# Tables of 65, 88 and 106 rows padded to 128 in DRAM, and the transforms moved one projection back, in a hybrid Hyena and RG-LRU block

## The chip, the cores and the metric

One core of one Trainium2 chip. The metric is the device time of one execution in microseconds (us), as the median of several runs. The core has a matrix engine (TensorE, PE), VectorE (DVE), ScalarE (ACT), GpSimd (POOL), and SyncE (SP), from whose queue nearly all transfers are issued; sixteen DMA engines move the data.

## What is computed

One layer on 528 positions (16 meta tokens and 512 tokens) of width 1024. Cut to what matters:

```
n    = rmsnorm(h)                                  # 528 x 1024
proj = n @ w_in                                    # hyena v, x1, x0 | rglru x | rglru gate | branch gates
A    = fft_long_conv(v * x1, filter) * x0          # two-sided, length 528, 512 channels
B    = (rglru(x, forward) + rglru(x, backward)) * gelu(gate)
h    = h + (sigmoid(gA) * (A @ hy_out) + sigmoid(gB) * (B @ rg_out)) @ w_out
h    = h + peer(rmsnorm(h))                        # product-key retrieval of experts
out  = rmsnorm(h)[16:]
```

The filter of the convolution comes from a small network (two sine layers of 64 on 528 positions, then 64 to 1024, times an exponential decay). The kernel does the Fourier transforms as matrix products with tables of cosines and sines.

## The kernel before, in words

**Precision and weights.** Every product is done with operands split into a high and a low f16 half: three matmuls for one (`mm3`, lines 84 to 88; lines 86, 87 and 88 are the three). A weight block of 128x1024 f32 (512 KB, `wf`) is loaded from SP's queue, split by ScalarE (line 81, the high half) and VectorE (line 82, the low half), and used by TensorE. `w_load`, `w_prep` and `w_get` (lines 94 to 122) keep this going: three `wf` buffers, so that a load waits until VectorE has split the block three before it, and splits that run two blocks ahead of the projection that asks. A projection's `w_get` puts these splits into ScalarE's and VectorE's queues; each engine works in the order in which its instructions were put there.

**Order of the front.** `front` (from line 284) writes the order out by hand. SP's queue begins with `hs` (the filter network's input and first weights, 65 rows), four parts of `xt` (the activations), the vectors, three `wf`, the identity, `w3` (65 rows) and `dec` (the decay, 106 rows). Then come the norm, and the projections in sequence, each followed by steps of background generators (`proj`, lines 256 to 282, whose last lines step the generators it was given):

- four pairs of projections for v and x1 (line 271, 48 matmuls of 264 columns each). The first pair is done together in both PSUM buffers of its kind, then the next weights are split, and only then are the two evacuated (`pad`, line 406). In the background: the filter network's second layer and `filter_taps` (lines 184 to 222), which multiplies by `dec` and leaves the split taps `pq` (j from 0 to 4, s for the sum and the difference of both directions).
- `filter_dft` (lines 224 to 248): five groups of 30 matmuls, each with its own table `kc` (106 rows), three buffers. The first two tables are asked for after the second pair, the other three when the groups begin. ScalarE evacuates a group (`kri`, line 246).
- four projections for x0, then eight for the gelu gates (24 matmuls of 512 columns each). Each takes one step of `hyena_conv` (lines 591 to 690) and one of `small_params`. The steps of `hyena_conv` are: load `ud` (88 rows) and `iv` (106 rows) and fold the input; three steps of transposes and their splits `eo` (line 612, by way of lines 81 and 82); five steps with a forward transform each (`fwd`, 18 matmuls, `ps_u`), the first of which also holds the last `eo` split, and each later one the product of the transform before (lines 628 to 633, then the split `ri`); the last product; four steps with an inverse transform each (`inv`, 30 matmuls of 264 columns, `ps_y`) and the post-processing of the one before; the last post-processing. The twelve projections take twelve of the fifteen steps; the rest is drained after the last one (lines 460 to 462).
- the RG-LRU projections and scans, the output projections, and then the expert stage (`peer`), which reads 128 expert blocks from two tables and gathers rows, to the end.

PSUM has two buffers for projections and two for everything else in the front (`pg`). The tables `kdft`, `udft`, `idft` and `dec` are made on the host in `constants` (line 1355), `hy_small` (for `hs` and `w3`) in `layout` (line 1397).

Of the kernel before, what the change touches and what calls it, by code (L numbers as in the profile page):

```python
# [8 lines left out]
F32 = mybir.dt.float32  # L9
F16 = mybir.dt.float16  # L10
# [10 lines left out]
L = SEQ + META  # L21
HL = L // 2
EPS = 1e-6
D_HY = 512
FFN = 64
# [3 lines left out]
FN = 5  # L29
FC = 106  # L30
NF = FN * FC
EC = 88
# [34 lines left out]
class Kernel:  # L67
# [156 lines left out]
    def filter_dft(self, p, psum, hy, pq, kri):  # L224
        nc, a = self.nc, self.a
        kcs = []

        def load(f):
            if f < FN:
                kc = p.tile([FC, 2, 2, FN, FC], F16, name="kc", bufs=3)  # L230
                nc.sync.dma_start(kc, a["kdft"][f])
                kcs.append(kc)
        for f in range(2):
            load(f)
        yield
        for f in range(FN):
            load(f + 2)
            kc = kcs[f]
            ps = psum.tile([128, 2, 512], F32, name="ps_kf", tag="pg")
            for s in range(2):  # L240
                for j in range(FN):
                    n = min(FC, L - j * FC)
                    self.mm3(ps[:FC, s, :], kc[:n, s, 0, j, :], kc[:n, s, 1, j, :],
                             pq[:n, s, 0, j, :], pq[:n, s, 1, j, :], j == 0, j == FN - 1)
            kr = hy.tile([FC, 2, D_HY], F32, name="kri", tag="kr", bufs=FN + 1)
            nc.scalar.activation(kr, ps[:FC], AF.Copy, scale=1.0 / (S_K * S_C))
            kri.append(kr)
            yield
# [35 lines left out]
    def front(self, xt, acc):  # L284
        nc, tc, a, keep = self.nc, self.tc, self.a, self.keep
        ctx = ExitStack()
        psum = ctx.enter_context(tc.tile_pool(name="psf", bufs=2, space=PSUM))
# [63 lines left out]
        kri = []  # L351
        pf = ctx.enter_context(ExitStack())
        fp = pf.enter_context(tc.tile_pool(name="filt", bufs=1, side="right"))
        hs = fp.tile([FFN + 1, L + 2 * FFN + 4], F32, name="hs")
        nc.sync.dma_start(hs, a["hy_small"][:, :L + 2 * FFN + 4])
        for c in range(0, 8, 2):
            nc.sync.dma_start(xt[:, c:c + 2, :], a["ht"][:, c:c + 2, :])
# [8 lines left out]
        h1 = fp.tile([FFN, L], F32, name="h1")  # L366
        h2 = fp.tile([FFN + 1, L], F32, name="h2")
        pq = fp.tile([FC, 2, 2, FN, D_HY], F16, name="pq")
        dec = fp.tile([FC, FN, D_HY], F32, name="dec")
        w3 = fp.tile([FFN + 1, 2 * D_HY], F32, name="w3")  # L370
        nc.sync.dma_start(w3, a["hy_small"][:, L + 2 * FFN + 4:])
        nc.sync.dma_start(dec, a["dec"])
        nc.gpsimd.memset(h2[FFN:FFN + 1, :], 1.0)
        mlp = [self.filter_mlp(fp, psum, i, hs, h1, h2) for i in range(2)]
# [40 lines left out]
        bg = self.filter_taps(fp, psum, w3, h2, pq, dec)  # L415
# [32 lines left out]
        sp = self.small_params()  # L448
        bg = self.hyena_conv(psum, hy, u, x0, kri, y_hy)
# [6 lines left out]
            nc.scalar.activation(t, ps[:, 0, :], AF.Gelu_apprx_tanh, scale=1.0 / (S_N * S_W))  # L456
            gelus.append(t)
        for i in range(8):
            self.proj(psum, False, ev_gelu, (bg, sp))
        self.flush_evac()  # L460
        for _ in bg:
            pass
# [8 lines left out]
        with tc.tile_pool(name="ru", bufs=1, side="right") as ru:  # L471
# [17 lines left out]
            bg = self.rglru(ru, psum, rgx, gelus, rgw, y_rg)  # L489
# [36 lines left out]
        for i in range(8):  # L526
            w = self.w_get(self.wi)
# [63 lines left out]
    def hyena_conv(self, psum, hy, u, x0, kri, y_hy):  # L591
        nc, tc, a = self.nc, self.tc, self.a
        with tc.tile_pool(name="hc", bufs=1, side="right") as p:
            ud = p.tile([EC, 2, 2, 3, NF], F16, name="ud")
            nc.sync.dma_start(ud, a["udft"])
            iv = p.tile([FC, 2, 2, FN, HL], F16, name="iv")
            nc.sync.dma_start(iv, a["idft"])
            eo = p.tile([EC, 2, 2, 3, D_HY], F16, name="eo")
            fold = []
            for i in range(4):  # L600
# [64 lines left out]
            for k in range(6):  # L665
# [4 lines left out]
                if k % 2 == 1:  # L670
                    yield
            post()
            post = None
            for f in range(FN):
                nxt = fwd(f)
# [673 lines left out]
def _hl(m, s):  # L1349
    m = np.asarray(m, np.float64) * s  # L1350
    hi = m.astype(np.float16)
    return hi, (m - hi.astype(np.float64)).astype(np.float16)


def constants():
    c = {}
    f = np.arange(NF)
    w = np.pi * f / L
    n = np.arange(NF)
    ok = (f[None, :] <= L)  # L1360
    kd = np.zeros((FC, 2, 2, FN, NF), np.float16)
    for s, fn in enumerate((np.cos, np.sin)):
        m = fn(n[:, None] * w[None, :]) * ok
        for r, v in enumerate(_hl(m, S_C)):
            kd[:, s, r] = v.reshape(FN, FC, NF).transpose(1, 0, 2)
    c["kdft"] = np.ascontiguousarray(kd.reshape(FC, 2, 2, FN, FN, FC).transpose(4, 0, 1, 2, 3, 5))
    m = np.arange(HL) + 0.5
    ud = np.zeros((EC, 2, 2, 3, NF), np.float16)
    iv = np.zeros((FC, 2, 2, FN, HL), np.float16)
    wt = np.where((f == 0) | (f == L), 1.0, 2.0) * (f <= L)  # L1370
    for s, fn in enumerate((np.cos, np.sin)):
        x = fn(m[:, None] * w[None, :]) * ok
        for r, v in enumerate(_hl(x, S_C)):
            ud[:, s, r] = v.reshape(3, EC, NF).transpose(1, 0, 2)
        y = (x * wt[None, :]).T
        for r, v in enumerate(_hl(y, S_C)):
            iv[:, s, r] = v.reshape(FN, FC, HL).transpose(1, 0, 2)
    c["udft"], c["idft"] = ud, iv
    t32 = np.linspace(0.0, 1.0, L, dtype=np.float32)[:, None]
    wz = np.float32(2.0 * math.pi / L) * np.arange(L, dtype=np.float32)[:, None]  # L1380
    bands = np.linspace(1e-4, 15, 16, dtype=np.float32)[None, :]
    ph = (bands * wz).astype(np.float64)
    z = np.concatenate([t32, np.cos(ph), -np.sin(ph)], axis=-1).astype(np.float32)
    zt = np.zeros((FFN + 1, L), np.float32)
    zt[:33] = z.T
    c["zt"] = zt
    deltas = np.abs(np.linspace(math.log(1e-2) / 0.3, math.log(1e-2) / 1.5, D_HY, dtype=np.float32))
    dec = np.zeros((NF, D_HY), np.float32)
    dec[:L] = np.exp((-t32 * deltas).astype(np.float64))
    c["dec"] = np.ascontiguousarray(dec.reshape(FN, FC, D_HY).transpose(1, 0, 2))  # L1390
    c["ident"] = np.eye(128, dtype=np.float32)
    c["iota"] = np.broadcast_to(np.arange(128, dtype=np.float16), (128, 128)).copy()
    c["iof"] = np.broadcast_to(np.repeat(np.arange(TOPK, dtype=np.float16), TOPK), (128, 256)).copy()
    return c


def layout(i):
    i = {k: np.asarray(v) for k, v in i.items()}
    a = {}
    h = np.concatenate([i["meta"], i["x"][0]], axis=0)  # L1400

    def cols(v):
        return np.ascontiguousarray(v.reshape(-1, 128).T)

    a["ht"] = np.ascontiguousarray(h.T.reshape(8, 128, L).transpose(1, 0, 2))
    a["vecs"] = np.concatenate([cols(i[k]) for k in VEC], axis=1)

    def lhs(w):
        k, m = w.shape
        return np.ascontiguousarray(  # L1410
            w.reshape(k // 128, 128, m // 128, 128).transpose(2, 1, 0, 3).reshape(m // 128, 128, k))

    a["gfb"] = np.broadcast_to(i["g_final"], (128, D)).copy()
    a["w_in"] = lhs(i["w_in"][0])
    a["hy_out"] = lhs(i["hy_out"][0])
    a["rg_out"] = lhs(i["rg_out"][0])
    a["w_out"] = lhs(i["w_out"][0])
    a["wq"] = lhs(i["peer_wq"][0])
    a["rg_gate_w"] = np.ascontiguousarray(
        i["rg_gate_w"][0].reshape(32, 128, 128).transpose(1, 0, 2).reshape(128, 32 * 128))  # L1420
    a["keys"] = np.ascontiguousarray(i["peer_keys"][0].reshape(16, 128, 128).transpose(2, 0, 1).reshape(128, 2048))
    a["peer_u"] = np.ascontiguousarray(
        i["peer_u"][0].reshape(128, 128, 8, 128).transpose(0, 3, 2, 1).reshape(128, 128, D))
    a["peer_v"] = np.ascontiguousarray(i["peer_v"][0].reshape(128, 128, D))
    a["peer_un"] = np.ascontiguousarray(i["peer_u"][0])

    def rows(v):
        return np.concatenate([v, np.zeros((FFN + 1 - v.shape[0], v.shape[1]), v.dtype)], axis=0)

    hb = np.stack([i["hy_b1"][0], i["hy_b2"][0], i["hy_freq"][0, 0], i["hy_freq"][0, 1]], axis=1)  # L1430
    c = constants()
    a["hy_small"] = np.concatenate(
        [c.pop("zt"), rows(i["hy_w1"][0]), rows(i["hy_w2"][0]), rows(hb),
         np.concatenate([i["hy_w3"][0], i["hy_b3"][0][None]], axis=0)], axis=1)
    a.update(c)
    return a

# [15 lines left out]
```

## Time and profile before

| | |
|---|---|
| median of 3 runs | 1748.39 us (1746.59 to 1750.73) |
| the profiled execution, its own time | 1748.05 us |
| its span, first to last instruction | 1746.3 us |
| mean granted TensorE clock | 0.975 of full speed |
| PE / DVE / ACT / POOL busy | 93% / 80% / 44% / 21% of the span |
| moved by DMA | 414.33 MB, 237 GB/s over the span |

The profile is of one execution. Busy shares are over the whole span; the stages differ. A row of a timeline gives the start, the duration, the engine, the line of the kernel, the operation, output<-input, shapes, the count and, in brackets, how long the engine was idle before it and what ended that wait. Matmuls overlap one another, so that the distance of two starts tells their pace, and not the duration of one. PEclk is the granted clock of TensorE as a share of 2.4 GHz, and the DMA share is the mean busy share of the sixteen DMA engines.

### The profile page before, as it was taken

To read this page: it belongs to the slowest core of one execution; us is meant where nothing else is said; L and a number is where in the kernel's file an instruction comes from. 1 tells how busy PE (TensorE), PEld (TensorE's weight loads), DVE (VectorE), ACT (ScalarE), POOL (GpSimd) and SP (SyncE) were. 2 spreads that over 40 slices of the span, in tenths; PEclk is the share of its full clock that TensorE was granted. 3 is DMA by queue.
4 is the path that set the end of the run, shared out by engine and by line. 5 is a ranking of instruction groups with operands and counts; after the bars stand their busy time and mean duration, and the time that the engine had idled before them with its cause. 6 is when DMAs were issued, how large, how long until landed. Compare 5 with 4: busy or idle time off the path is not lost. (4 is left out here: it accounts for less than half of the span.)

```text
span 1746.3 us, 25010 instructions
## 1 busy us (share of the span) xinstructions
PE 1630.6 (93%) x9451; PEld 910.5 (52%) x9451; DVE 1403.7 (80%) x2422; ACT 767.6 (44%) x1055; POOL 359.8 (21%) x321
## 2 busy tenths in 40 slices
PE   6987999899989988898999998899999999999898
PEld 4755576544434544565665665455554444444343
DVE  5825768997567899899899797688889999989884
ACT  4323349893243432443654675333333333333342
POOL 0000000000000000222222123344444444444410
PEclk8998999999999999999999999899999999999999
DMA  4214132123323345778787799999999999999981
GB/s 164 93 48 120 63 106 75 61 85 92 114 82 99 97 124 193 244 241 288 272 311 278 282 341 349 340 388 323 344 370 359 402 396 404 399 395 406 395 299 49
DMA packets 134541, 414.33 MB, mean 237 GB/s; under 512 B 11955, under 2 KB 39859, under 8 KB 131047
## 3 DMA queue, kind: packets, MB, share of 16 engines
q1 hardware_dynamic: 97347, 277.87, 45.3%
q0 software_dynamic: 37072, 134.86, 20.6%
q8 instruction: 74, 1.21, 0.3%
q14 instruction: 48, 0.39, 0.1%
HBM read 366.54 MB, written 46.14 MB: 236 GB/s over the span
## 5 line engine op out<-in xcount | busy, mean ns | idle before, releaser
L978 PE MATMUL ob<-wh,pt 128*128 128x512 f16 x2304 | 512.1, 380 | 20.8 <-DVE wh L82 12.0
L82 DVE SCALAR_TENSOR_TENSOR wh<-wf,wh 128x1024 f16<-128x1024 f32 (+1 forms) x340 | 409.3, 1207 | 135.8 <-ACT wh L81 133.3
L81 ACT ACTIVATE wh<-wf 128x1024 f16<-128x1024 f32 (+1 forms) x340 | 352.6, 1041 | 176.6 <-DMA wf<-in_peer_v 58.4
L978 PEld LDWEIGHTS <-pt 128*128 128x128 f16 x2304 | 225.9, 98 | 290.1 <-issue 24.2
L88 PE MATMUL ps_e<-x,wh 128*128 128x384 f16 x1024 | 337.7, 330 | 16.2 <-DVE wh L82 16.2
L86 PE MATMUL ps_e<-x,wh 128*128 128x384 f16 x1024 | 338.2, 330 | 2.3 <-ACT gs L952 2.3
L87 PE MATMUL ps_e<-x,wh 128*128 128x384 f16 x1024 | 337.9, 330 | 0.0
L1092 POOL DMA_INDIRECT rows<-in_peer_un,gidx x128 | 181.4, 1417 | 447.7 <-DVE junk L1125 396.0
L88 PEld LDWEIGHTS <-wh 128*128 128x128 f16 x1504 | 148.6, 99 | 150.1 <-DVE wh L82 23.6
L87 PEld LDWEIGHTS <-wh 128*128 128x128 f16 x1504 | 148.7, 99 | 130.7 <-issue 13.8
L1092 POOL DMA_INDIRECT rows<-in_peer_v,gidx x128 | 171.8, 1342 | 196.5 <-DVE acc L1146 157.4
L86 PEld LDWEIGHTS <-wh 128*128 128x128 f16 x1504 | 148.8, 99 | 121.6 <-issue 6.0
L1146 DVE SCALAR_TENSOR_TENSOR acc<-rows,dots,acc 128x1024 f32<-128x1024 f32 x127 | 162.7, 1281 | 19.2 <-DMA rows<-in_peer_v,gidx 18.3
L940 ACT ACTIVATE pt<-pf 128x384 f16<-128x384 f32 x128 | 66.5, 520 | 218.4 <-DVE pf L933 162.3
L1125 DVE SCALAR_TENSOR_TENSOR junk<-rows,xn 128x1024 f32<-128x1024 f32 x128 | 156.1, 1219 | 4.8 <-DMA rows<-in_peer_un,gidx 4.1
L271 PE MATMUL ps_p<-n,wh 128*128 128x264 f16 x960 | 115.3, 282 | 8.2 <-ACT pad L406 6.8
L271 PEld LDWEIGHTS <-wh 128*128 128x128 f16 x960 | 95.7, 100 | 28.5 <-issue 10.3
L952 ACT ACTIVATE gs<-ps_e 128x384 f32<-128x384 f32 x96 | 47.0, 489 | 133.7 <-PE ps_e L88 124.8
L1287 ACT ACTIVATE stg<-ps_gt 128x512 f32<-128x512 f32 x96 | 93.1, 1082 | 14.1 <-PE ps_gt L1280 10.5
L944 DVE TENSOR_TENSOR pt<-pf,pt 128x384 f16<-128x384 f32 x128 | 70.8, 553 | 12.4 <-ACT pt L940 12.4
L86 PE MATMUL ps_p<-n,wh 128*128 128x512 f16 x192 | 74.0, 386 | 0.0
L87 PE MATMUL ps_p<-n,wh 128*128 128x512 f16 x192 | 73.8, 384 | 0.0
(276 smaller groups left out, 1840.1 us busy)
## 6 DMA issues: line engine op xcount, KB each, us to landing
wf<-in_peer_u SPq DMA_DIRECT2D x128, 512.0 KB
wf<-in_peer_v SPq DMA_DIRECT2D x128, 512.0 KB
gd<-stg SPq DMA_DIRECT2D x24, 1024.0 KB
wf<-in_w_in SPq DMA_DIRECT2D x44, 512.0 KB
gin<-gd SPq DMA_DIRECT2D x7, 3072.0 KB
sd<-gs SPq DMA_DIRECT2D x48, 384.0 KB
sin<-sd SPq DMA_DIRECT2D x48, 384.0 KB
wf<-in_wq SPq DMA_DIRECT2D x16, 512.0 KB
```

Of the source, the lines that this page charges most:

```text
L81: self.nc.scalar.activation(hi, src, AF.Copy, scale=s)
L82: self.nc.vector.scalar_tensor_tensor(lo, src, s, hi, op0=OP.mult, op1=OP.subtract)
L86: mm(ps, lh, rh, start=first, stop=False)
L87: mm(ps, lh, rl, start=False, stop=False)
L88: mm(ps, ll, rh, start=False, stop=last)
L271: nc.tensor.matmul(ps[:, h, :HL], x, n[:, y, c, h * HL:(h + 1) * HL], start=(c == 0 and x is lh and y == 0), stop=(c == 7 and x is ll))
L944: nc.vector.tensor_tensor(pt[i][:, 1, :], pf.pop(i), pt[i][:, 0, :], OP.subtract)
L978: mm(ob[tt][:, h, :], pp[:, x, sl], w[:, y, h * 512:(h + 1) * 512], start=first and k == 0, stop=last and k == 2)
L1092: self.nc.gpsimd.indirect_dma_start(out=r, out_offset=None, in_=table, in_offset=bass.IndirectOffsetOnAxis(ap=self.gidx[:, j:j + 1], axis=0))
L1125: nc.vector.scalar_tensor_tensor(junk, rows.pop(0), 1.0, self.xn, op0=OP.mult, op1=OP.mult, accum_out=self.dots[:, j:j + 1])
L1146: nc.vector.scalar_tensor_tensor(acc2, r, d, acc2, op0=OP.mult, op1=OP.add)
L1287: nc.scalar.activation(st[c][:, :, o:o + 4].rearrange("p e t -> p t e"), ps, AF.Copy, scale=S_P / S_G)
```

## The change

The four tables are padded with zero rows to 128 in DRAM, and so is `hy_small`; the tiles that they are loaded into have 128 rows, and each load takes the whole table. The computation reads the same rows as before (`w3`, `ud` and `iv` are cut to their rows after the load; the others are addressed by rows already).

`hyena_conv` gets one more step: the last `eo` split is a step of its own, so that the first forward transform comes one projection later. The gelu projections from the fifth on take two steps each, so that all sixteen steps are done when the last projection is. Counted from the last x0 projection, the order on TensorE before was: gelu 0, transform 0, gelu 1, transform 1, gelu 2, transform 2, gelu 3, transform 3, gelu 4, transform 4, gelu 5, gelu 6, inverse 0, gelu 7, inverses 1, 2, 3. After: gelu 0, gelu 1, transform 0, gelu 2, transform 1, gelu 3, transform 2, gelu 4, transforms 3 and 4, gelu 5, inverse 0, gelu 6, inverses 1 and 2, gelu 7, inverse 3.

```diff
--- before.py
+++ after.py
@@ -227,7 +227,7 @@
 
         def load(f):
             if f < FN:
-                kc = p.tile([FC, 2, 2, FN, FC], F16, name="kc", bufs=3)
+                kc = p.tile([128, 2, 2, FN, FC], F16, name="kc", bufs=3)
                 nc.sync.dma_start(kc, a["kdft"][f])
                 kcs.append(kc)
         for f in range(2):
@@ -351,7 +351,7 @@
         kri = []
         pf = ctx.enter_context(ExitStack())
         fp = pf.enter_context(tc.tile_pool(name="filt", bufs=1, side="right"))
-        hs = fp.tile([FFN + 1, L + 2 * FFN + 4], F32, name="hs")
+        hs = fp.tile([128, L + 2 * FFN + 4], F32, name="hs")
         nc.sync.dma_start(hs, a["hy_small"][:, :L + 2 * FFN + 4])
         for c in range(0, 8, 2):
             nc.sync.dma_start(xt[:, c:c + 2, :], a["ht"][:, c:c + 2, :])
@@ -366,9 +366,10 @@
         h1 = fp.tile([FFN, L], F32, name="h1")
         h2 = fp.tile([FFN + 1, L], F32, name="h2")
         pq = fp.tile([FC, 2, 2, FN, D_HY], F16, name="pq")
-        dec = fp.tile([FC, FN, D_HY], F32, name="dec")
-        w3 = fp.tile([FFN + 1, 2 * D_HY], F32, name="w3")
+        dec = fp.tile([128, FN, D_HY], F32, name="dec")
+        w3 = fp.tile([128, 2 * D_HY], F32, name="w3")
         nc.sync.dma_start(w3, a["hy_small"][:, L + 2 * FFN + 4:])
+        w3 = w3[:FFN + 1]
         nc.sync.dma_start(dec, a["dec"])
         nc.gpsimd.memset(h2[FFN:FFN + 1, :], 1.0)
         mlp = [self.filter_mlp(fp, psum, i, hs, h1, h2) for i in range(2)]
@@ -456,7 +457,7 @@
             nc.scalar.activation(t, ps[:, 0, :], AF.Gelu_apprx_tanh, scale=1.0 / (S_N * S_W))
             gelus.append(t)
         for i in range(8):
-            self.proj(psum, False, ev_gelu, (bg, sp))
+            self.proj(psum, False, ev_gelu, (bg, sp) + (bg,) * (i >= 4))
         self.flush_evac()
         for _ in bg:
             pass
@@ -591,10 +592,11 @@
     def hyena_conv(self, psum, hy, u, x0, kri, y_hy):
         nc, tc, a = self.nc, self.tc, self.a
         with tc.tile_pool(name="hc", bufs=1, side="right") as p:
-            ud = p.tile([EC, 2, 2, 3, NF], F16, name="ud")
+            ud = p.tile([128, 2, 2, 3, NF], F16, name="ud")
             nc.sync.dma_start(ud, a["udft"])
-            iv = p.tile([FC, 2, 2, FN, HL], F16, name="iv")
+            iv = p.tile([128, 2, 2, FN, HL], F16, name="iv")
             nc.sync.dma_start(iv, a["idft"])
+            ud, iv = ud[:EC], iv[:FC]
             eo = p.tile([EC, 2, 2, 3, D_HY], F16, name="eo")
             fold = []
             for i in range(4):
@@ -670,6 +672,7 @@
                 if k % 2 == 1:
                     yield
             post()
+            yield
             post = None
             for f in range(FN):
                 nxt = fwd(f)
@@ -1388,6 +1391,11 @@
     dec = np.zeros((NF, D_HY), np.float32)
     dec[:L] = np.exp((-t32 * deltas).astype(np.float64))
     c["dec"] = np.ascontiguousarray(dec.reshape(FN, FC, D_HY).transpose(1, 0, 2))
+
+    for k, ax in (("kdft", 1), ("udft", 0), ("idft", 0), ("dec", 0)):
+        w = [(0, 0)] * c[k].ndim
+        w[ax] = (0, 128 - c[k].shape[ax])
+        c[k] = np.pad(c[k], w)
     c["ident"] = np.eye(128, dtype=np.float32)
     c["iota"] = np.broadcast_to(np.arange(128, dtype=np.float16), (128, 128)).copy()
     c["iof"] = np.broadcast_to(np.repeat(np.arange(TOPK, dtype=np.float16), TOPK), (128, 256)).copy()
@@ -1432,6 +1440,7 @@
     a["hy_small"] = np.concatenate(
         [c.pop("zt"), rows(i["hy_w1"][0]), rows(i["hy_w2"][0]), rows(hb),
          np.concatenate([i["hy_w3"][0], i["hy_b3"][0][None]], axis=0)], axis=1)
+    a["hy_small"] = np.pad(a["hy_small"], ((0, 128 - FFN - 1), (0, 0)))
     a.update(c)
     return a
```

## Rows read from the trace of the kernel before

**Rows 1.** The page, the span in 40 equal slices: busy share of the DMA engines, in tenths.

```profile
DMA  4214132123323345778787799999999999999981
```

**Rows 2.** Waits of TensorE, 0 to 260 us: in total, times, longest.

```profile
PE ps_u L86 <- ACT eo L81: 8.8, 1, 8.8
...
PE ps_kf L86 <- DMA kc<-in_kdft: 5.0, 2, 4.1
```

**Rows 3.** Timeline of ScalarE: start, duration, work, idle before and what ended it.

```profile
39.92 1.06 ACT L81 ACTIVATE wh<-wf 128x1024 f16<-128x1024 f32 x1 [8.26 <-DMA wf<-in_w_in]
40.88 0.59 ACT L406 ACTIVATE pad<-ps_p 128x528 f32<-128x528 f32 x1
...
164.93 1.06 ACT L81 ACTIVATE wh<-wf 128x1024 f16<-128x1024 f32 x1 [14.82 <-DMA wf<-in_w_in]
```

**Rows 4.** DMA issues: what, queue, count, size of each.

```profile
kc<-in_kdft SPq DMA_DIRECT2D x5, 438.9 KB
...
iv<-in_idft SPq DMA_DIRECT2D x1, 1093.1 KB
dec<-in_dec SPq DMA_DIRECT2D x1, 1060.0 KB
...
hs<-in_hy_small SPq DMA_DIRECT2D x1, 167.6 KB
```

**Rows 5.** Stretches: us, engines' busy time, then granted clock, DMA share, GB/s.

```profile
10.00:12.00 2.00, 2.00 (x6) 1.50 (x5) 0.71 (x1) 0.94 (x3) 0.00 (x0) 1.00 1.01 414
...
108.00:112.00 4.00, 4.00 (x20) 2.40 (x19) 0.00 (x0) 0.34 (x1) 0.00 (x0) 1.00 0.13 53
156.00:160.00 4.00, 3.02 (x14) 1.65 (x13) 0.00 (x0) 0.00 (x0) 0.00 (x0) 1.00 0.12 53
...
102.20:107.20 5.00, 5.00 (x12) 2.56 (x13) 0.00 (x0) 0.00 (x0) 0.00 (x0) 0.50 0.13 53
```

**Rows 6.** Timeline of SP's queue: when tables are issued.

```profile
89.80 8.48 SPq L231 DMA_DIRECT2D kc<-in_kdft  x3
...
129.86 0.25 SPq L597 DMA_DIRECT2D iv<-in_idft  x1
```

**Rows 7.** Timeline of TensorE: 96 projection matmuls, at three places.

```profile
21.64 13.09 PE L271 MATMUL ps_p<-n,wh 128*128 128x264 f16 x96
...
41.53 13.32 PE L271 MATMUL ps_p<-n,wh 128*128 128x264 f16 x96 [6.81 <-ACT pad L406]
...
236.87 10.97 PE L271 MATMUL ps_p<-n,wh 128*128 128x264 f16 x96
```

**Rows 8.** Timeline: the filter transform's first matmul, and a split that it needs.

```profile
84.88 0.38 PE L86 MATMUL ps_kf<-pq,kc 106*106 106x512 f16 x1
...
85.23 0.69 DVE L82 SCALAR_TENSOR_TENSOR pq<-kp,pq 104x512 f16<-104x512 f32 x1 [0.70 <-ACT pq L81]
```

**Rows 9.** Timeline of ScalarE: evacuations after the third and fifth filter groups.

```profile
111.66 1.02 ACT L246 ACTIVATE kri<-ps_kf 106x1024 f32<-106x1024 f32 x1 [12.59 <-PE ps_kf L88]
...
125.73 1.02 ACT L246 ACTIVATE kri<-ps_kf 106x1024 f32<-106x1024 f32 x1 [6.56 <-PE ps_kf L88]
```

**Rows 10.** Timeline of TensorE: first matmuls of forward transforms 0, 1 and 2.

```profile
155.61 0.38 PE L86 MATMUL ps_u<-eo,ud 88*106 88x512 f16 x1
...
176.73 0.38 PE L86 MATMUL ps_u<-eo,ud 88*106 88x512 f16 x1
...
185.80 0.38 PE L86 MATMUL ps_u<-eo,ud 88*106 88x512 f16 x1
```

**Rows 11.** Timeline of VectorE: a product's start, its split, and a weight split.

```profile
208.03 0.69 DVE L628 TENSOR_TENSOR yt<-ps_u,kri 106x512 f32<-106x512 f32 x1 [2.00 <-PE ps_u L88]
...
211.81 1.29 DVE L82 SCALAR_TENSOR_TENSOR ri<-yt,ri 106x512 f16<-106x512 f32 x2
213.35 1.23 DVE L82 SCALAR_TENSOR_TENSOR wh<-wf,wh 128x1024 f16<-128x1024 f32 x1 [0.25 <-ACT wh L81]
```

## The prediction

> **What bounds the kernel now.** TensorE is busy most of the span, and the page's forty slices show the DMA engines near their limit only in the last half [rows 1]. The changed tables are used in the front, the first 250 us, where those engines mostly idle: a wait for a table there can't come from a full memory system. Second I read the list of waits on TensorE up to 260 us: `ps_u` behind ScalarE's `eo` (8.8 us) and `ps_kf` behind the load of `kc` (5.0 us) [rows 2]; a third, 6.81 us, stands before the matmuls at 41.53 [rows 7]. Third, ScalarE's timeline says why two of them exist though they name no DMA: a weight split waited 8.26 us and another 14.82 us for `wf`, and what TensorE needed (`pad`, `eo`) was queued behind it [rows 3].
>
> Why should a `wf` be late when its load is small? Fourth, the stretches. At 108 to 112 and at 156 to 160 us one table alone is moving (`kc`, then `iv`), and the sixteen DMA engines are busy 0.13 and 0.12 of the time at 53 GB/s; at 10 to 12 us, with loads of 128 rows under way, they are all busy (1.01) at 414 GB/s [rows 5]. 0.125 is two engines of sixteen. So I read: a load of 106 rows runs on two engines, and each later load, which has a share on those two, waits behind it. The sizes fit: `kc` is 438.9 KB, 449 thousand bytes, 8.5 us at 53 GB/s; `iv` 21 us, `dec` 20.5 us [rows 4].
>
> **The padding, stall by stall.**
>
> *`dec`, start of the projections.* TensorE ends the first 96 matmuls at 21.64+13.09 = 34.73 and starts again at 41.53 [rows 7], because the `pad` evacuation at 40.88 stands behind the late split [rows 3]. With `dec` on sixteen engines that `wf` is there when ScalarE asks at 39.92-8.26 = 31.7; `pad` then starts at the end of the matmuls, and TensorE 0.65 us later as now, at 35.4: 6.15 us. The next 96 matmuls took 13.32 us, against 10.97 for 96 of the same kind with no pause ahead of them [rows 7]: 2.35 us more for TensorE if the pause goes. But VectorE and ScalarE, whose chain from here to the filter transform has few pauses, gain only the 6.15. What is late next is `pq`: its low half, 85.23+0.69 now, comes at 79.8, while TensorE, 8.5 us earlier than now, wants it 13 matmuls of 0.216 us (rate below) after 84.88-8.5, at 79.2 [rows 8]. With the hand-over that costs 0.7 us: 7.8 us.
>
> *`kc`.* Three of the five tables are issued from 89.80 on [rows 6], in order. A group of 30 matmuls at 0.216 us takes 6.48 us, so ScalarE, after an evacuation of 1.02 us, should wait 5.46 for the next; before the third and the fifth it waits 12.59 and 6.56 [rows 9]: 7.13+1.10 = 8.2 us, idle and slow matmuls together. After: `wf` and `kc`, 1 MB, take 2.5 us at 414 GB/s, 5 at half that; the third group wants it at 111.66-12.59-1.02 = 98.05 in today's times, 8 us after the issue, and both ends move together. Covered; 8.2 us gained.
>
> *`ud`, `iv`.* From the first matmul of transform 0 to that of transform 1 are 21.12 us; from 1 to 2, the same 42 matmuls, 9.07, that is 0.216 each [rows 10]. So 12.05 us go. Padding and reordering serve the same stall: the split that holds up `eo` waited 14.82 us and TensorE only 8.8 [rows 2, 3], so without the late `wf` `eo` is there 6 us before it is wanted, and the added projection (24 x 0.216 = 5.2 us) makes that 11. Counted once.
>
> *Added bytes.* `hs` grows from 65 to 128 rows, 167.6 KB to 330 [rows 4], ahead of `xt` in the queue, and the norm waits for `xt`: 162 KB at 414 GB/s are 0.4 us. Bounds: 0 (it also spreads wider) and 0.8 (half the rate). I take 0.4, by the nearest row. `w3` and `dec` stand behind `xt` and before a `wf` wanted only at 31.7: nothing; without that cover 0.47 MB more, 1.1 us. `ud` and `iv`, issued up to 129.86 [rows 6], are 3 MB when padded, 7 us, before a `wf` wanted at 164.93-14.82 = 150.1 [rows 3]: nothing. Slicing the tiles by rows costs no instruction.
>
> **The reordering.** The new yield moves each transform one projection back, and from the fifth gelu projection on two steps follow each. These steps issue no DMA and nothing on POOL, so SP's order stays; on ScalarE and VectorE they pass weight splits and gelu evacuations. (a) Transforms 3 and 4 run back to back, and the product of 4 has one projection left before the first inverse. A product takes VectorE from 208.03 to 211.81+1.29 = 213.1, its first low half ready after 4.45; a weight split adds 1.23 and its wait 0.25 [rows 11]. Counted from the end of transform 3, that half is ready at 5.3+1.5+4.45 = 11.3; TensorE wants it after 3.9 (transform 4), 5.2 and 13 matmuls of 264 columns at 10.97/96 = 0.114, at 10.6. Cost 0.7 us; bounds 0 and 2.2 (a second split in between). (b) The last gelu evacuation now stands behind the last inverse's post-processing and frees a buffer for the second RG-LRU projection, 5.5 us after: nothing, at most 1. (c) That projection's weight split passes behind two post-processings and still has a gelu projection and an inverse to spare: nothing.
>
> **Sum.** 7.8 + 8.2 + 12.05 - 0.4 - 0.7 = 26.95 us. The profiled execution took 1748.05 (span 1746.3): 1721.1; it stood 0.34 under the median of the runs: 1721.4. Behind the front all work waits for the front's result, and weights come through three buffers, so nothing is fetched sooner that could collide, and the shift passes through whole.
>
> **Rivals.**
>
> *Slower: the rate belongs to these tables, not to their row count.* If such a load gets 53 GB/s at any count, padding stretches it by 128/106. `dec` lands 4.3 us later, three `kc` in a row 5.3, `iv` 4.4, which the added projection hides: 9.6 us slower, 1758. It decides if the padded loads still show a share of 0.13. Against: 128-row loads in the same queue [rows 5]. Chance 0.05. The Trainium skill, "DMA: Bandwidth & Descriptors", section on why a DMA increments its semaphore by 16, gives a DMA the largest number of engines up to 16 that divides its rows: 2 for 106, 11 for 88, 13 for 65, 16 for 128. The trace agrees with the 2.
>
> *No table was late: bytes alone set a load's time, and the waits have another cause.* Then nothing comes back, and `hs` and the reordering cost 0.4+0.7: 1749.5. Against: `kc` was issued from 89.80 and its user was held about 12 us [rows 6, 9], while 414 GB/s would bring it in one. Chance 0.02. The Trainium skill, "DMA: Bandwidth & Descriptors", section on the anatomy of one DMA, has such a rule: about 2.0 us and bytes over 436 GB/s, by which an estimate for `kc` is 3.0 us, and 3.2 padded. The trace disagrees by a factor of four.
>
> *The clock stays down.* After the `kc` pause the granted clock was 0.50 from 102.2 to 107.2 [rows 5], 1.2 GHz. If it falls in these places without the pauses, only idle time comes back; the gain loses 1.65 + (8.2-5.0) + (12.05-8.8) = 8.1 us: 1729.5. Against: matmuls with no pause ahead ran at 0.216 us throughout [rows 10]. Chance 0.1.
>
> *The gain becomes slack.* The last half is near the DMA's limit [rows 1]; if something there kept its own time, the result would be 1748. Against: its loads start only when the front's buffers come free. Chance 0.02.
>
> **Numbers.** Forecast 0.81: 1721.4, and by the bounds above, with a pause more or less that brings the clock down elsewhere (2.35 us, [rows 7]), 1715 to 1728. To hold 8 in 10 the range reaches into the clock's case: 1715 to 1731. 0.2%, about what a measurement of this kernel can tell, is 3.5 us: faster 0.91, same 0.04, slower 0.05.
>
> **What would show it.** Right: no wait for `kc`; no wait of ScalarE over 3 us for `wf` before 200 us; a DMA share near 1 for a few us at each table instead of 0.13 for 8 to 30; the RG-LRU projections from about 210 us instead of 236.87 [rows 7]. Wrong: a share of 0.13 beside padded tables; a new wait of TensorE over 2 us for `pq` or before the first inverse; RG-LRU 27 us earlier, but the end not.

## The result, and the profile after

| | before | after |
|---|---|---|
| median | 1747.49 us (4 runs) | 1717.99 us (4 runs, 1715.17 to 1720.26) |
| the profiled execution, its own time | 1748.05 us | 1716.81 us |
| its span | 1746.3 us | 1715.0 us |
| mean granted clock | 0.975 | 0.982 |

The ratio is 0.9834, 95% interval 0.9817 to 0.9851: 29.5 us faster. The forecast was 1721.4 in a range of 1715 to 1731.

The list of waits on TensorE in the changed kernel, 0 to 245 us (total, times, longest):

```profile
PE ps_f L178 <- ACT h L182: 4.7, 1, 4.7
PE ps_f L178 <- DMA hs<-in_hy_small: 4.1, 1, 4.1
PE ps_p L271 <- DVE wh L82: 2.0, 1, 2.0
PE ps_t L612 <- DVE eo L82: 0.5, 1, 0.5
PE ps_kf L87 <- DVE pq L82: 0.3, 1, 0.3
PE ps_y L88 <- DVE ri L82: 0.3, 1, 0.3
...
```

The waits of 8.8 and 5.0 us [rows 2] and the one of 6.81 [rows 7] are gone. The first four lines stood in the list before too (4.7, 3.4, 1.4 and 0.5 us). In place of the stalls stand the two small ones that the forecast had expected, for `pq` and before an inverse transform, at 0.3 us each.

The timeline of TensorE after, at the places of [rows 7, 8, 10] (start, duration, work):

```profile
20.43 23.05 PE L271 MATMUL ps_p<-n,wh 128*128 128x264 f16 x192
...
73.57 0.38 PE L86 MATMUL ps_kf<-pq,kc 106*106 106x512 f16 x1
...
106.54 10.63 PE L271 MATMUL ps_p<-n,wh 128*128 128x264 f16 x93
...
141.81 0.38 PE L86 MATMUL ps_u<-eo,ud 88*106 88x512 f16 x1
...
150.87 0.38 PE L86 MATMUL ps_u<-eo,ud 88*106 88x512 f16 x1
...
206.40 10.96 PE L271 MATMUL ps_p<-n,wh 128*128 128x264 f16 x96
```

The first two groups of 96 matmuls are now one row of 192, without a pause that the list of waits shows. From transform 0 to transform 1 there are 9.06 us instead of 21.12. The RG-LRU projections begin at 206.40 instead of 236.87, 30.5 us earlier, and the span is 31.3 shorter: what the front gained has arrived at the end.

ScalarE's timeline after, at the places of [rows 3, 9]:

```profile
29.41 1.99 ACT L81 ACTIVATE wh<-wf 128x1024 f16<-128x1024 f32 x2
31.85 0.61 ACT L407 ACTIVATE pad<-ps_p 128x528 f32<-128x528 f32 x1 [0.45 <-PE ps_p L271]
...
93.78 1.02 ACT L246 ACTIVATE kri<-ps_kf 106x1024 f32<-106x1024 f32 x1 [5.46 <-PE ps_kf L88]
...
106.74 1.02 ACT L246 ACTIVATE kri<-ps_kf 106x1024 f32<-106x1024 f32 x1 [5.46 <-PE ps_kf L88]
```

Two weight splits run back to back where 8.26 us lay between them, `pad` waits only for its own matmuls, and the third and fifth evacuations wait the 5.46 us of an undisturbed group.

The stretches of the changed kernel where `dec` moves (14 to 16 us) and where `ud` and then `iv` move (113 to 117, 117 to 119); the last three columns are the granted clock, the DMA share and GB/s:

```profile
14.00:16.00 2.00, 0.00 (x0) 0.00 (x0) 1.79 (x3) 1.39 (x2) 0.00 (x0) 0.94 1.08 455
...
113.00:117.00 4.00, 4.00 (x38) 3.48 (x36) 2.43 (x3) 0.60 (x1) 0.13 (x2) 1.00 1.00 426
...
117.00:119.00 2.00, 2.00 (x20) 1.85 (x18) 0.39 (x1) 1.02 (x2) 0.00 (x0) 1.00 1.00 428
```

The share of 0.13 at 53 GB/s [rows 5] has become 1.0 or a little over at 426 to 455.

To place the gain, I cut the span at five points of TensorE's timeline: the first projection, the first filter tap (`ps_k`, 54.69 before and 43.31 after), the first filter transform, the first x0 projection (125.53 before), the first RG-LRU projection. The same table serves for the experiments. Every number is the length of a stretch in us, from that run's profile. Below, "the `kc` stretch" is the column of the filter transforms, and "the transforms' stretch" the one with x0, gelu and hyena.

| run | start | pairs (`dec`) | taps | filter transforms (`kc`) | x0, gelu, hyena (`ud`, `iv`) | rest | span |
|---|---|---|---|---|---|---|---|
| before | 21.64 | 33.05 | 30.19 | 40.65 | 111.34 | 1509.4 | 1746.3 |
| after | 20.43 | 22.88 | 30.26 | 32.97 | 99.86 | 1508.6 | 1715.0 |
| padding alone | 21.45 | 23.57 | 30.26 | 32.97 | 99.30 | 1505.4 | 1712.9 |
| order alone | 21.08 | 32.05 | 30.20 | 40.59 | 112.02 | 1507.0 | 1742.9 |
| 112, 96, 80 rows | 21.42 | 22.95 | 30.26 | 32.98 | 99.86 | 1507.4 | 1714.9 |
| 122 rows | 21.30 | 37.00 | 30.19 | 47.27 | 114.77 | 1502.4 | 1752.9 |
| `dec` alone | 20.92 | 24.27 | 30.25 | 42.90 | 111.64 | 1512.9 | 1742.9 |
| `kc` alone | 21.30 | 32.36 | 30.20 | 32.41 | 112.22 | 1508.3 | 1736.8 |
| `iv` alone | 21.29 | 33.96 | 30.20 | 40.50 | 99.29 | 1509.0 | 1734.2 |
| `hs`, `w3`, `ud` alone | 20.68 | 34.55 | 30.20 | 41.86 | 107.17 | 1509.3 | 1743.8 |
| 120 and 104 rows | 21.05 | 23.16 | 30.25 | 32.97 | 99.85 | 1507.1 | 1714.4 |

The rest, which nothing here touches, lies between 1502 and 1513, so the total of a single profile is good to some 5 us only. A stretch in which no wait is left comes out alike to a tenth of a microsecond (taps; 32.97; 99.86); one with a wait varies by up to 1 us between profiles, and the pairs by 1.4 to 2.5. The times below are medians of repeated runs.

### The profile page after: what moved, and what is told of

Same layout as the page of the kernel before. It is cut to its first block, busy times and chain, and to the rows that moved or that the text cites. A ratio compares the mean times of both kernels' runs of the same rounds, so it can differ in the third digit from the quotient of the medians.

```text
span 1715.0 us, 25010 instructions
## 1 busy us (share of the span) xinstructions
PE 1619.6 (94%) x9451; PEld 905.7 (53%) x9451; DVE 1402.8 (82%) x2422; ACT 767.4 (45%) x1055; POOL 368.9 (22%) x321
## 5 line engine op out<-in xcount | busy, mean ns | idle before, releaser
L981 PE MATMUL ob<-wh,pt 128*128 128x512 f16 x2304 | 511.9, 380 | 19.2 <-DVE wh L82 11.8
L1095 POOL DMA_INDIRECT rows<-in_peer_v,gidx x128 | 180.1, 1407 | 187.3 <-DVE acc L1149 154.9
L87 PEld LDWEIGHTS <-wh 128*128 128x128 f16 x1504 | 148.3, 99 | 129.5 <-issue 12.1
L1290 ACT ACTIVATE stg<-ps_gt 128x512 f32<-128x512 f32 x96 | 93.1, 1083 | 15.8 <-PE ps_gt L1283 10.5
```

Source lines behind the costliest of these rows:

```text
L87: mm(ps, lh, rl, start=False, stop=False)
L981: mm(ob[tt][:, h, :], pp[:, x, sl], w[:, y, h * 512:(h + 1) * 512], start=first and k == 0, stop=last and k == 2)
L1095: self.nc.gpsimd.indirect_dma_start(out=r, out_offset=None, in_=table, in_offset=bass.IndirectOffsetOnAxis(ap=self.gidx[:, j:j + 1], axis=0))
L1290: nc.scalar.activation(st[c][:, :, o:o + 4].rearrange("p e t -> p t e"), ps, AF.Copy, scale=S_P / S_G)
```

## The experiments

The theory: a load runs on as many of the sixteen DMA engines as divide its row count (two for 106 and for 122 rows), and holds up, on these, every load issued later. The rivals: the new order is what helps; any padding, or bytes, or a place in the queue is what matters.

**Padding without the new order.** The changed kernel with these two places as before:

```diff
-            self.proj(psum, False, ev_gelu, (bg, sp) + (bg,) * (i >= 4))
+            self.proj(psum, False, ev_gelu, (bg, sp))
...
             post()
-            yield
             post = None
             for f in range(FN):
```

> All tables padded to 128 rows, the order of the steps as before. If the stalls came from loads that ran on two engines, the padding alone gives the whole: 1716 to 1719 us, no wait of TensorE for `eo` in transform 0, RG-LRU projections from 206 us within 1. If the added projection is needed to cover `eo`, transform 0 still waits for it by 2 us or more and the time is 1720 to 1729.

Measured: 1715.62 us (1714.64 to 1716.65), ratio to the kernel before 0.9819 (0.9805 to 0.9832). Transform 0 waits for nothing. The whole gain is the padding's. The transforms' stretch is 99.30 us, against 99.86 with the new order: the order costs 0.56 us, too little for the total to show (the intervals of the two kernels overlap). RG-LRU begins at 207.55, a little outside what was expected, because the start was 1 us later.

**The new order without padding.** The opposite edit: the kernel before, with the added step and the second step per projection.

> The new order of the steps alone, tables of 65, 88 and 106 rows as before. If the late weight block is the cause, the order gives nothing: gelu projection 1 needs the PSUM buffer of the last x0 projection, whose evacuation stands behind the late split, so it waits as transform 0 did, and the 14 matmuls that ran before that wait now wait too: 0 to 4 us slower than before, 1747 to 1752. If the order covers the stall, 5 us or more are gained: 1742 or less.

Measured: 1745.33 us (11 runs), ratio 0.9990 (0.9978 to 1.0001): no difference that can be told, and just below the expected band. The profile shows the mechanism that was expected, in the transforms' stretch, which is 0.7 us longer. TensorE's wait, from its list of waits:

```profile
PE ps_p L86 <- ACT pad L406: 10.5, 1, 10.5
```

And the late split, from ScalarE's timeline:

```profile
163.06 1.06 ACT L81 ACTIVATE wh<-wf 128x1024 f16<-128x1024 f32 x1 [14.56 <-DMA wf<-in_w_in]
```

The wait has changed its name and not its cause. Instead of transform 0 for `eo`, it is gelu projection 1 that stands, 10.5 us, for the evacuation of the last x0 projection, which is queued on ScalarE behind the same late split.

**Fewer rows, still multiples of sixteen.**

```diff
-                kc = p.tile([128, 2, 2, FN, FC], F16, name="kc", bufs=3)
+                kc = p.tile([112, 2, 2, FN, FC], F16, name="kc", bufs=3)
...
-            ud = p.tile([128, 2, 2, 3, NF], F16, name="ud")
+            ud = p.tile([96, 2, 2, 3, NF], F16, name="ud")
...
```

> The changed kernel with 112 rows in place of 128 for the 106-row tables, 96 for `ud`, 80 for `hs` and `w3`: all multiples of sixteen, fewer bytes. If a load runs on as many engines, up to sixteen, as divide its rows, the time is that of the changed kernel, 0 to 1 us less, and the loads show a share near 1. If only a full 128 rows spread, the stalls are back: 1740 or more.

Measured: 1716.30 us, ratio 0.9821 (0.9807 to 0.9836), the stretches as after. A full 128 rows are not needed to remove the stalls. But the loads did not run as expected: the share was 0.99 and only 245 GB/s moved (the last section).

**Padding to a bad number.** The 106-row tables padded to 122 rows, 2 x 61, in the old order.

```diff
-                kc = p.tile([FC, 2, 2, FN, FC], F16, name="kc", bufs=3)
+                kc = p.tile([122, 2, 2, FN, FC], F16, name="kc", bufs=3)
...
```

> The order as before, and only the 106-row tables padded, to 122 rows (2 x 61). If the count of engines is a divisor of the rows, it stays at two and each load carries 15% more: `dec` lands 3.1 us later, three `kc` 3.9, `iv` 3.2, so 6 to 12 us slower than before, 1753 to 1759, with a share of 0.13 beside them. If rows near 128 spread, or any padding helps, the time is 1717 to 1722.

Measured: 1758.10 us, ratio 1.0067 (1.0052 to 1.0082), 10 to 12 us slower than before. Stretches of this kernel in which a table alone is moving (`kc`, then `iv`), and TensorE's waits:

```profile
116.00:120.00 4.00, 3.61 (x17) 2.19 (x18) 0.00 (x0) 0.96 (x1) 0.00 (x0) 1.00 0.13 52
168.00:172.00 4.00, 1.25 (x6) 0.64 (x5) 0.00 (x0) 0.00 (x0) 0.00 (x0) 1.00 0.12 53
```

```profile
PE ps_u L86 <- ACT eo L81: 11.6, 1, 11.6
PE ps_p L271 <- ACT pad L406: 9.7, 1, 9.7
PE ps_kf L86 <- DMA kc<-in_kdft: 8.5, 3, 5.0
```

Share and rate are those of 106 rows, and all three waits have grown. The stretches grew by 3.95, 6.6 and 3.4 us where 3.1, 3.9 and 3.2 were expected; the `kc` stretch by more: 3.5 us more of waiting, and some 3 us because TensorE, which had stood for `kc`, ran at the lower clock a second time in it (after the wait before the fifth group; before, only after the third):

```profile
126.20:132.20 6.00, 6.00 (x15) 2.97 (x16) 0.00 (x0) 0.00 (x0) 0.00 (x0) 0.50 0.00 0
```

Padding helps by the number that it reaches and not by being padding. This was also the forecast's rival on the slower side, made real: at 53 GB/s each added row costs time.

**One table at a time**, each in the old order. `dec`:

```diff
-        dec = fp.tile([FC, FN, D_HY], F32, name="dec")
+        dec = fp.tile([128, FN, D_HY], F32, name="dec")
```

> Only `dec` padded to 128 rows, everything else as before. If the first stall is `dec` alone on two engines, the stretch from the first projection to the filter taps falls from 33.05 to about 23 us, the 6.8 us wait is gone, and the stretches of `kc` (40.65) and of the transforms (111.3) stay within 0.5: 8 to 11 us faster, 1737 to 1740. If the stalls hand the delay on, less than 4 us arrive at the end.

Measured: 1738.00 us, ratio 0.9952 (0.9936 to 0.9967). The pairs' stretch fell to 24.27 and the wait is gone. One thing was missed: the `kc` stretch grew by 2.25 us. Its user now comes earlier and waits 6.5 us in place of 5.0, and `pq`, which was in time before, costs 0.6:

```profile
PE ps_kf L86 <- DMA kc<-in_kdft: 6.5, 2, 5.7
```

So part of one gain is given back at the next table as long as that one is still slow.

`kc`:

> Only `kc` padded to 128 rows. The filter transforms' stretch falls from 40.65 to 32.4 (five groups of 6.48 us, no wait) and the others stay: 8 us faster, 1738 to 1742. If the waits for `kc` come from its place in the queue and not from its two engines, the stretch stays over 38.

Measured: 1738.44 us, ratio 0.9954 (0.9937 to 0.9970); the stretch is 32.41, five undisturbed groups. The transforms' stretch is 0.9 us longer, which is within the scatter of a stretch with a wait.

`iv`:

```diff
-            iv = p.tile([FC, 2, 2, FN, HL], F16, name="iv")
+            iv = p.tile([128, 2, 2, FN, HL], F16, name="iv")
```

> Only `iv` padded to 128 rows; `ud` stays at 88 rows. If the late weight block waited for `iv` on its two engines, `eo` is in time, the stretch of the transforms falls from 111.3 to about 99.3 as with all tables padded in the old order: 11 to 13 us faster, 1735 to 1738. If `ud` shares the blame, transform 0 still waits by 2 us or more.

Measured: 1735.59 us, ratio 0.9933 (0.9908 to 0.9958); the stretch is 99.29 and no wait for `eo` is left. Curing this one table was enough to remove the whole stall of 12 us.

The three single gains are 0.48, 0.46 and 0.67%, together 1.61%, against 1.81% with all tables padded: they add up within their intervals.

**The tables that ran on many engines.** `hs` and `w3` (65 rows) and `ud` (88) to 128, the 106-row tables as before.

> Only `hs`, `w3` (65 rows) and `ud` (88) padded to 128; the 106-row tables as before. If only the loads with 106 rows were the trouble, all three waits stay and the time is that of before within 3 us, the start up to 0.8 us later for the added bytes. If every table below 128 rows cost something, 2 us or more are gained.

Measured: 1742.90 us, ratio 0.9976 (0.9962 to 0.9991): some 4 us faster, where nothing was expected if the 106-row loads alone were the trouble. The stretches show where: the transforms' fell by 4.2 us, and the wait for `eo` from 8.8 to 4.6:

```profile
PE ps_p L271 <- ACT pad L407: 8.5, 1, 8.5
PE ps_kf L86 <- DMA kc<-in_kdft: 5.5, 3, 3.5
...
PE ps_u L86 <- ACT eo L81: 4.6, 1, 4.6
```

So the load of `ud`, with 88 rows, does bear on that stall, although it ran on more than two engines (the run pads three tables, but of these only `ud` is loaded near this stretch). `iv` stands behind it in the queue: in the packed trace of the kernel before (its records of single rows on their way), the rows of `ud` move from 131.9 to 139.7 us and those of `iv` from 139.0 to 163.2; here they move from 133.4 to 137.9 and from 137.6 to 160.7. Counted from the issue of `ud`, `iv` ends 4.2 us sooner. Padding `ud` is not needed once `iv` is cured, as the run before showed. The start (20.68) is in the scatter of all runs: the added bytes of `hs` can't be seen.

## Why the prediction was right, and by how much each step was off

**The cause.** Right, and shown from both sides: 112, 120 and 128 rows remove the stalls, 122 rows make them longer, and the share beside the 106-row and 122-row loads is 0.12 to 0.13. That a later load is held on two engines alone can be seen directly in the kernel before. The weight block that came 14.82 us late [rows 3] and the two issued after it have 128 rows each. In the packed trace 336 of their 384 rows move by 150.9 us, that is 112 for a block, or 14 engines at eight rows; the other 48, 16 for a block, move only from 161.4 us on, as `iv` ends. Two stretches, the first while the third of these blocks moves beside `iv`, the second while all three stand unfinished:

```profile
148.60:150.90 2.30, 1.82 (x15) 1.28 (x14) 2.06 (x4) 0.59 (x1) 0.00 (x0) 1.00 1.01 234
152.00:161.00 9.00, 7.02 (x33) 3.55 (x32) 0.04 (x1) 0.00 (x0) 0.00 (x0) 1.00 0.13 54
```

**`dec`.** The forecast was 8.5 us for TensorE (6.15 of the pause and 2.35 of the second 96 matmuls) and then 0.7 lost at `pq`. The pairs' stretch fell by 10.2. Measured from start to start of matmuls, the second 96 gained 2.36, as forecast. The pause gave 6.8: it was wrong that TensorE would still stand 0.65 us behind `pad`. `pad` does not wait for the last of the 96 matmuls; it starts at 31.85 us, the last of them at 32.21 and the next group at 32.51, so that only 0.2 us are lost. The remaining 1.0 us is in no term of the sum: the first 96 matmuls, from the start of the first to that of the last, took 11.8 us instead of 12.8. The granted clock says why. Before at 22 to 26 us, after at 20 to 24:

```profile
22.00:24.00 2.00, 2.00 (x11) 1.24 (x9) 1.93 (x4) 0.70 (x2) 0.00 (x0) 0.50 0.14 61
24.00:26.00 2.00, 2.00 (x11) 1.34 (x10) 1.97 (x4) 0.84 (x2) 0.00 (x0) 0.52 0.12 51
```

```profile
20.00:22.00 2.00, 2.00 (x9) 0.98 (x8) 1.93 (x4) 1.06 (x3) 0.00 (x0) 0.50 0.02 8
22.00:24.00 2.00, 2.00 (x18) 1.62 (x16) 1.93 (x4) 1.04 (x2) 0.00 (x0) 0.85 0.00 0
```

In both, TensorE had stood 4.7 us for the filter network, and the clock was at 0.50 (1.2 GHz, the lower level) when the projections began. It was back some 2 us after their start in the changed kernel, and over 4 us after in the kernel before. This is not the change's doing as far as the runs tell: in the runs with `dec` padded the first 96 matmuls took 11.8 to 13.2 us, in the others 12.1 to 13.3, while the second 96 took 10.7 in every run with `dec` padded. So this 1.0 us was luck.

**`kc`.** 8.2 us forecast; with `kc` alone padded the stretch fell by 8.24. With all tables padded it fell by 7.7, because the wait for `pq` stands in it: 0.56 us, where 0.7 was forecast with the hand-over to the matmul (the list's 0.3 is the wait without it).

**`ud`, `iv`.** 12.05 less 0.7 for the order were forecast; the stretch fell by 11.48. Size and cause were right: padding alone gives 12.04, and `iv` alone 12.05. What the forecast missed is inside the cause: it laid the lateness on `iv`'s two engines alone, but a faster load of `ud` also takes 4.2 us off the stall, since `iv` then starts sooner. The two gains don't add up: with `iv` cured nothing is left for `ud`.

**The order.** 0.7 us forecast for the first inverse behind the product of transform 4; 0.56 measured, all of it at that inverse (3.94 us from its first matmul to the next projection, 3.38 with padding alone). That padding and order serve the same stall was right for the padding. It was wrong for the order: alone it covers nothing, because the added projection needs a buffer behind the same split. The same holds for the 4.4 us of `iv` that the prediction's slower rival took to be hidden by the added projection.

**Added bytes.** 0.4 us forecast for `hs`. It lands 0.6 us later (TensorE's wait 3.42 before, 4.05 after), but nothing follows from it: the start scatters from 20.4 to 21.6 with and without padding.

**Sum.** 26.95 forecast; 31.3 in the spans. Of the 4.3 between, 0.6 is the hand-over at `pad` that did not come; 1.0 is the first stretch's clock, 1.6 the start and 0.8 the rest, and these three are scatter as far as the other runs show. The medians stand 29.5 apart. The range was wider below than its working: the terms that it names (0.4, 0.7 and 2.35) reach from 1721.4 down to 1718.0, and the last 3 us to 1715 have none. The median of 1717.99 lies just at that edge.

**The rivals.** "The rate belongs to these tables" fell with the share and rate of the padded loads. "No table was late" fell with the waits. (The 3.0 us that the prediction estimates for `kc` from the Trainium skill, "DMA: Bandwidth & Descriptors", section on the anatomy of one DMA, comes from a fit given there for loads issued from GpSimd. These loads are issued from SP's queue, so the factor of four is no evidence against that page.) "The clock stays down" fell too: the granted clock stays at 1.00 through all three places (for instance 113 to 119 us above). The gain did not become slack: the rest of the span is unchanged within its scatter.

## What to carry to other kernels

Look at the DMA share beside a load that lands late. A small constant fraction, an eighth here, suggests that it runs on a few engines, and what is issued behind it may then be late too, under other names (here `pad` and `eo` on ScalarE). Choose row counts for tables by how they divide, best a full 128 rows, and pad with zeros if need be; a wrong padding (122) makes it worse. Where a wait is named after an engine, follow the queue of that engine to what stands before it before reordering work around it: the new order alone moved the wait to another place and gained nothing.

## What the runs showed of the hardware that was not expected

Many engines are not the same as a high rate. Stretches in which `ud` is most of what moves, in turn: before (88 rows), the version with 96 and 112 rows (96), the one with 120 and 104 rows (104), the one with `hs`, `w3` and `ud` padded (128); share and GB/s stand last:

```profile
133.50:139.50 6.00, 6.00 (x56) 5.33 (x55) 2.79 (x6) 2.50 (x4) 0.13 (x2) 1.00 0.74 160
```

```profile
115.00:119.00 4.00, 4.00 (x38) 3.56 (x37) 1.50 (x3) 0.00 (x0) 0.13 (x2) 1.00 0.99 245
119.00:123.00 4.00, 4.00 (x39) 3.51 (x36) 3.06 (x6) 3.33 (x5) 0.00 (x0) 1.00 0.96 248
```

```profile
115.50:119.50 4.00, 4.00 (x38) 3.59 (x37) 0.82 (x3) 0.63 (x2) 0.13 (x2) 1.00 0.95 209
```

```profile
133.50:137.50 4.00, 4.00 (x38) 3.49 (x36) 2.67 (x5) 0.82 (x2) 0.13 (x2) 1.00 1.00 421
```

Divided by sixteen engines and the share, one busy engine moves 13.5 GB/s with 88 rows, 15.5 with 96, 13.8 with 104 and 26.3 with 128. The second row of the 96-row version is its `iv` of 112 rows, as slow. The two engines of a 106-row load reach 53/(16 x 0.125) = 26.5 each. The packed traces say the same of single rows: one row of `ud` (12720 bytes) takes 962 ns at the median with 88 rows, 808 with 96, 952 with 104 and 476 with 128. One row of `dec` (10240 bytes) takes 385 ns with 106 rows or 128, 710 with 112 and 727 with 120. So for these tables a load on two engines and one of 128 rows run at some 26 GB/s per engine, and those in between, on many engines, at about half. It is no rule for every load: a row of `hs` (2640 bytes) takes 106 ns with 65, 80, 104 and 128 rows alike, 25 GB/s.

The last run was made to see whether it is enough that each engine has a group of eight rows, as with 128.

```diff
-                kc = p.tile([128, 2, 2, FN, FC], F16, name="kc", bufs=3)
+                kc = p.tile([120, 2, 2, FN, FC], F16, name="kc", bufs=3)
...
-            ud = p.tile([128, 2, 2, 3, NF], F16, name="ud")
+            ud = p.tile([104, 2, 2, 3, NF], F16, name="ud")
...
```

> The changed kernel with 120 rows (15 x 8) for the 106-row tables and 104 (13 x 8) for `ud`, `hs` and `w3`. With 128 rows, `ud` and `iv` moved at 424 to 470 GB/s; with 96 and 112 rows (16 x 6, 16 x 7) the engines were as busy but moved 229 to 258, and 88 rows (11 x 8) 154 at a share of 0.70. If each engine's rows must be a group of eight, these loads run at 380 to 430 GB/s at a share of 0.9 or more, and the 88 rows were slow for another reason. If any count but 128 is slow, they run at 200 to 270. All stalls stay covered either way: 1714 to 1720.

Measured: 1717.95 us, ratio 0.9842 (0.9805 to 0.9879); the load of 104 rows at 209 GB/s. Groups of eight rows are not enough. What halves the rate stays open: no run here separates the memory's side from the receiving one. Here the stalls are covered either way, and the versions with 112 and 120 rows can't be told from the changed kernel; where such a load is waited for, 128 rows are the safe choice, even with a fifth more bytes.
